# P times V as fp32 products of two heads in different columns of the array, V kept whole in the place of the norm rows, and single banks for column products

## The chip, the cores and the metric

The kernel runs on one core of a Trainium2 chip. The metric is the device time of one execution in microseconds (us); lower is better. The engines are TensorE (PE, with its weight loads PEld), VectorE (DVE), ScalarE (ACT), GpSimd (POOL) and the DMA queue of SyncE (SP). SBUF is the on-chip memory, PSUM the small memory into which PE writes; PSUM has eight banks here of 512 fp32 values in each of 128 partitions.

## The reference

Two layers on 256 tokens of width 1024, all in fp32. Layer 0 mixes tokens with a gated MLP (gMLP), layer 1 with attention in 16 heads of 64; after each mixer comes a gated MLP with a causal convolution of width 3 (ConvFFN, width 2816). Every part ends in `x <- LayerNorm(alpha * x + f(x))`. Since one attention block holds 256 tokens, attention sees its own block alone: plain causal attention with a bias by distance.

```python
def chunked_gmlp(x, w_in, ln_g, ln_b, w_s, b_s, w_out):
    z = jax.nn.gelu(x @ w_in)
    u, v = jnp.split(z, 2, axis=-1)
    v = layer_norm(v, ln_g, ln_b)
    ...
    sv = jnp.einsum('gts,bnsgc->bntgc', w, v) + b_s.T[None, None, :, :, None]
    return (u * sv.reshape(B, S, GMLP_WIDTH)) @ w_out
...
        p = jax.nn.softmax(logits, axis=-1)
        ...
        return (jnp.einsum('bhqjl,bhqjld->bhqd', p_sel, v_sel)
                + jnp.einsum('bhql,bhld->bhqd', p_own, v_own))
    ...
    return o @ w_o

def conv_ffn(x, w_up, conv_w, conv_b, w_down):
    h = x @ w_up
    ...
    return (jax.nn.gelu(g) * val) @ w_down
```

## The kernel before

**Products in parts.** An fp32 matrix is cut into a high part in the rounded type fp32r and a low part, the rest. ACT makes the high part by a copy (line 338 of the profile, `act`), DVE the low part by a subtraction (line 344, `tt`); `split` records both. A product is then three fp32r products: high by high, high by low, low by high (line 326, `mms`). Small products are done in plain fp32 without parts: gMLP's spatial products and the part of the scores that needs it. In the trace an fp32 product shows as two records. Transposes are on line 332.

**Weights** arrive in chunks of 1 MB by SP (line 355), two raw places and five chunks ahead (`prep`, `spent`); a chunk is loaded when the one five before it is spent. ACT and DVE split each chunk into `whi` and `wlo`.

**The order of work.** The class `Plan` records every operation with its engine, an assumed duration and what it depends on, and then lists them for each engine by due times. The main products keep the order in which they are recorded; operations with `fill=True` (spatial products, scores, transposes, P times V) are slipped in as soon as they are ready. `plan.later(ns, fn)` records something only when PE's recorded work has gone on by so many ns; the constant `REST` does so with the last part of a layer norm (`rest` in `ln_back`: times and plus the norm rows), whose rows `lnrow` are loaded by `ln_rows` into a single place (`rowring`).

**PSUM.** Four banks are tiles of their own, `bank0` to `bank3`; the other four are the halves of two double tiles, `twos0` and `twos1`. `bank()` gives the oldest free single bank (a half of a double tile if none is free), `half()` a half of the double tile that was used longest ago, `couple(j)` names both halves of tile j, `taken(i, long)` takes a certain one. Dependences are kept per tile: a product into one half of a double tile waits for readers of the other half.

**Stages.** gMLP: v by rows, then u in eight groups g of 24 column products (`cols_times`, 256 columns each; the result is 128 features by 256 tokens) read by ACT's gelu; three groups later `spatial(g)`, two fp32 products of 128 columns in a half, read by DVE. Then a_out, the ConvFFN f_up0 and f_dn0 (`project_out`). Attention (`moba`): V by rows into the two couples, then for each pair i of heads (i = 0 to 7) `project(i, 0)` for Q and `project(i, 1)` for K, 24 column products each in a half; `scores(i - 1)`, two heads in different rows of the array (64 each), an fp32 product of 128 columns and three fp32r products of 256 for each head; `softmax`, whose first step is four DVE reads of the scores with the bias (line 825); `turn(i - 2)`, three transposes of P for each head; `apply(i - 3)`, P times V. Here P and V are both split, P's parts lie in `rr`; three products of 512 columns take both heads' P against 128 features of V, and three of 256 columns the second half of the tokens, so of the 128 by 512 result only each head's own 64 rows count. Two splits of 64 partitions take them out for b_o. Behind the last pair b_o and the second ConvFFN follow.

Of the kernel before, what the change touches and what calls it, by code (L numbers as in the profile page):

```python
# [13 lines left out]
AF = mybir.ActivationFunctionType  # L14
# [4 lines left out]
P = 128  # L19
D = 1024  # L20
# [25 lines left out]
T1_WAITS = (2600, 3300, 4000, 4700)  # L46
REST = 25000
AHEAD = 12000
# [175 lines left out]
def trunk_kernel(ctx: ExitStack, tc: tile.TileContext, a: dict, out: bass.AP):  # L224
# [64 lines left out]
    def couple(j):  # L289
        return j + BANKS // 2, j + BANKS // 2 + len(twos)  # L290
# [227 lines left out]
    def ln_back(r, st, mean, rstd, rows, t, li, h, l, waits):  # L518
# [16 lines left out]
        def turn(k0):  # L535
            pt, x32 = bank(), (x32a if step == 4 else x32b).new()
            transposes([(pt.ap[:, j * P:(j + 1) * P], x[:, (k0 + j) * P:(k0 + j + 1) * P]) for j in range(step)],
                       [(r, range(k0 // 2, (k0 + step) // 2))], [pt])
            for j in range(step):
                k = k0 + j  # L540
                act(x32.ap[:, j * P:(j + 1) * P], pt.ap[:, j * P:(j + 1) * P], AF.Identity, [pt, lncol], [(x32, [j])],
                    bias=lc[:, li, 1, k:k + 1], scale=lc[:, li, 0, k:k + 1], psum=True)
            parts = [(t, k) for k in range(k0, k0 + step)]
            split((h, parts, xt_view(h)[:, t, k0:k0 + step, :]), (l, parts, xt_view(l)[:, t, k0:k0 + step, :]),
                  (x32, range(step), x32.ap.rearrange("p (k c) -> p k c", k=step)))
            if k0 + step == KT:
                plan.later(REST, rest)

# [34 lines left out]
    def project_out(name, nk, at, xold, li, rows_i):  # L583

        rows = ln_rows(rows_i)
        last = li is None


# [17 lines left out]
        for t in range(NT):  # L606
# [17 lines left out]
            if t == NT - 1:  # L624
                for k in range(start, nk, 2):
                    spent(name, k // 2)

            st, mean, rstd = stats(r, x, cuts[t], lambda j, o, n: add(*mine[j], 1.0 if mine[j] in ends else ALPHA))
            if last:
# [9 lines left out]
    def gmlp():  # L639
# [37 lines left out]
        for g in range(GROUPS):  # L677
            b = half()
            cols_times(b, xh, xl, *sub("a_u", g // 2, g % 2))
# [78 lines left out]
    def moba(h, l, scr):  # L758
        n4 = KT * S
        oh, ol = place("rr", 0, n4), place("rr", n4, n4)  # L760
        vh, vl = place("rr", 2 * n4, NT * D), place("rr", 2 * n4 + NT * D, NT * D)
        pw = 2 * (P + S)
        pring = [Places("rr", [4 * n4 + (2 * j + x) * pw for x in range(2)], pw) for j in range(2)]
        qkring = [Places("ff", (j * 2 * P, j * 2 * P + P), P) for j in range(2)]
# [3 lines left out]
        ohv, olv = (b.ap.rearrange("p (k s) -> p k s", k=KT) for b in (oh, ol))  # L768
        vhv, vlv = (b.ap.rearrange("p (t d) -> p t d", t=NT) for b in (vh, vl))
        at = xt_at(h, l)  # L770
        pieces = [[(o, HALF, taken(i, True)) for o, i in zip((0, HALF), couple(j))] for j in range(NT)]
        for ks in (range(5), range(5, KT)):
            for t in range(NT):
# [6 lines left out]
                if ks[0]:  # L780
                    for o, n, b in pieces[t]:
                        parts = [(t, i) for i in range(o // P, (o + n) // P)]
                        split((vh, parts, vhv[:, t, o:o + n]), (vl, parts, vlv[:, t, o:o + n]), (b, [0], b.ap), psum=True)
                        done_with(b)
        held, biases = {}, {}

        def project(i, j):
            b, t = half(), qkring[j].new()
            cols_times(b, h, l, *sub("b_qk", i, j))
# [15 lines left out]
        def scores(i):  # L805
            ((q0, qh, ql), (k0, kh, kl)), bias = held[i], biases[i]
            bank2 = [bank() for _ in range(2)]

# [29 lines left out]
        def turn(i):  # L838
            ph, pl = (x.new() for x in pring)
            for hh in range(2):  # L840
                e, b = held[i][hh], bank()

                transposes([(b.ap[:, c * P:(c + 1) * P], e.ap[:, c * P:(c + 1) * P]) for c in range(3)],
                           [(e, [0, 1])], [b])
                sl = slice(hh * (P + S), (hh + 1) * (P + S))
                split((ph, [hh], ph.ap[:, sl]), (pl, [hh], pl.ap[:, sl]), (b, [0], b.ap[:, :P + S]), psum=True)
            held[i] = ph, pl

        def apply(i):
            ph, pl = held[i]  # L850
            b = bank()
            o3 = b.ap.rearrange("p (a b) -> p a b", a=2)
            vs = slice(i * P, (i + 1) * P)
            seq = [(vhv, ph), (vhv, pl), (vlv, ph)]
            w = [(o3, v[:, 0, vs], p.ap.rearrange("p (a s) -> p a s", a=2)[:, :, :S], j == 0, False)
                 for j, (v, p) in enumerate(seq)]
            w += [(o3[:, :, P:], v[:, 1, vs], p.ap.rearrange("p (a s) -> p a s", a=2)[:, :, S:], False, j == 2)
                  for j, (v, p) in enumerate(seq)]
            mms(w, [(vh, [(0, i), (1, i)]), (vl, [(0, i), (1, i)]), (ph, [0, 1]), (pl, [0, 1])], [b], fill=True)
            for hh in range(2):  # L860
                hs = slice(hh * DH, (hh + 1) * DH)
                split((oh, [(i, hh)], ohv[hs, i, :]), (ol, [(i, hh)], olv[hs, i, :]), (b, [0], o3[hs, hh, :]), psum=True)

# [108 lines left out]
```

## Time and profile before

| what | us |
|---|---|
| median of 3 executions | 578.51 (577.9 to 579.87) |
| the profiled execution | 579.16 |
| its span, first to last instruction | 577.5 |
| PE busy | 560.1 (97% of the span) |
| PEld busy | 485.9 |
| DVE busy | 473.7 |
| ACT busy | 361.9 |

The profile is of one execution. A row of the timeline gives the start, the duration, the engine, the line, what is written and read, and in brackets how long the engine was idle ahead of it and what ended that; neighbours of the same kind are joined (x2, x3). Ends of products on PE are modelled and overlap the next start, so steps are read from start to start. The granted clock was 0.997 of full speed on the mean. All times in the text are us from the start of the span, unless said otherwise.

### The profile page before, as it was taken

To read this page: it belongs to the slowest core of one execution; us is meant where nothing else is said; L and a number is where in the kernel's file an instruction comes from. 1 tells how busy PE (TensorE), PEld (TensorE's weight loads), DVE (VectorE), ACT (ScalarE), POOL (GpSimd) and SP (SyncE) were. 2 spreads that over 40 slices of the span, in tenths; PEclk is the share of its full clock that TensorE was granted. 3 is DMA by queue.
4 is the path that set the end of the run, shared out by engine and by line. 5 is a ranking of instruction groups with operands and counts; after the bars stand their busy time and mean duration, and the time that the engine had idled before them with its cause. 6 is when DMAs were issued, how large, how long until landed. Compare 5 with 4: busy or idle time off the path is not lost.

```text
span 577.5 us, 8559 instructions
## 1 busy us (share of the span) xinstructions
PE 560.1 (97%) x3210; PEld 485.9 (84%) x3210; DVE 473.7 (82%) x885; ACT 361.9 (63%) x660; POOL 11.3 (2%) x17
## 2 busy tenths in 40 slices
PE   6998999999999999999999999999999999999994
PEld 4798888888888878888889998888888888888884
DVE  5587989999999997558878889879999999996426
ACT  5555567776677685435568777658777778785300
POOL 0020010000000000001000000000000000000001
PEclk9999999999999999999999999999999999999998
DMA  7887544537454567742663442515456555567202
GB/s 260 330 336 274 199 145 151 215 145 259 188 211 156 210 230 267 259 169 87 250 250 117 181 165 92 201 73 183 183 188 254 199 170 211 219 218 255 110 1 73
DMA packets 20133, 110.93 MB, mean 192 GB/s; under 512 B 2251, under 2 KB 6268, under 8 KB 7676
## 3 DMA queue, kind: packets, MB, share of 16 engines
q1 hardware_dynamic: 20092, 110.39, 53.0%
q8 instruction: 25, 0.41, 0.3%
q14 instruction: 16, 0.13, 0.1%
HBM read 109.31 MB, written 1.07 MB: 191 GB/s over the span
## 4 chain that ended last, share of the span: by engine, by line
PE 92%; DVE 3%; DMA 2%; ACT 2%; issue 0%; SPq 0%; DVEq 0%; ACTq 0%
PE twos L326 60%; PE bank L326 29%; DMA raw<-in_a_v 2%; PE bank L332 2%; DVE wlo L344 1%; DVE rr L344 1%; ACT ff L338 1%; DVE x L348 0%; ACT whi L338 0%; ACT rr L338 0%; SPq L355 0%; DVE ff L825 0%; PE twos L332 0%; DVE ff L834 0%; DVE stat L494 0%
## 5 line engine op out<-in xcount | busy, mean ns | idle before, releaser
L326 PE MATMUL twos<-xt,whi 128*128 128x512 f32 (+1 forms) x1024 | 295.1, 354 | 2.0 <-ACT ff L338 1.5
L344 DVE TENSOR_TENSOR wlo<-raw,whi 128x1024 fp32r<-128x1024 f32 (+1 forms) x212 | 228.4, 1098 | 30.8 <-ACT whi L338 30.3
L326 PE MATMUL twos<-xt,wlo 128*128 128x256 f32 x832 | 231.5, 278 | 0.0
L338 ACT ACTIVATE whi<-raw 128x1024 fp32r<-128x1024 f32 (+1 forms) x212 | 195.0, 954 | 56.7 <-DMA raw<-in_f_up 18.2
L326 PEld LDWEIGHTS twos<-xt,whi 128*128 128x128 f32 x1024 | 179.5, 189 | 31.7 <-ACT ff L338 2.4
L326 PEld LDWEIGHTS twos<-xt,wlo 128*128 128x128 f32 x832 | 156.8, 188 | 0.1
L326 PE MATMUL bank<-whi,rr 128*128 128x512 f32 x432 | 135.2, 391 | 0.4 <-DVE smax L825 0.4
L326 PEld LDWEIGHTS bank<-whi,rr 128*128 128x128 f32 x432 | 81.1, 188 | 18.0 <-issue 0.6
L326 PE MATMUL bank<-wlo,rr 128*128 128x512 f32 x216 | 84.1, 389 | 0.0
L348 DVE SCALAR_TENSOR_TENSOR ff<-ff,convc 128x255 f32<-128x255 f32 (+1 forms) x160 | 69.1, 477 | 0.0
L338 ACT ACTIVATE ff<-twos 128x512 f32<-128x512 f32 (+2 forms) x64 | 31.4, 491 | 53.4 <-PE twos L326 52.6
L326 PEld LDWEIGHTS bank<-wlo,rr 128*128 128x128 f32 x216 | 40.6, 188 | 8.1
L338 ACT ACTIVATE ff<-ff,convc 128x256 f32<-128x256 f32 x80 | 45.5, 592 | 2.9 <-DVE ff L344 2.5
L344 DVE TENSOR_TENSOR ff<-twos,ff 128x512 f32<-128x512 f32 (+1 forms) x48 | 30.9, 645 | 16.0 <-ACT ff L338 11.7
L326 PE MATMUL twos<-whi,xt 128*128 128x512 f32 x128 | 42.1, 396 | 0.5 <-DVE x L348 0.5
L338 ACT ACTIVATE ff<-bank,lncol 128x128 f32<-128x128 f32 x48 | 18.9, 460 | 29.1 <-PE bank L332 28.4
L348 DVE SCALAR_TENSOR_TENSOR x<-x,bank 128x512 f32<-128x512 f32 x16 | 11.0, 686 | 23.7 <-PE bank L326 23.6
L326 PEld LDWEIGHTS twos<-whi,xt 128*128 128x128 f32 x128 | 24.1, 188 | 5.7 <-DVE x L348 0.9
L326 PE MATMUL bank<-whi,xt 128*128 128x512 f32 x64 | 21.9, 420 | 5.1 <-DVE xt L361 5.0
L338 ACT ACTIVATE rr<-ff 128x256 fp32r<-128x256 f32 x52 | 21.0, 406 | 7.4 <-DVE ff L344 7.4
L326 PE MATMUL twos<-wlo,xt 128*128 128x512 f32 x64 | 25.0, 390 | 0.0
L344 DVE TENSOR_TENSOR ff<-ff 128x256 f32<-128x256 f32 x52 | 21.6, 418 | 0.5 <-ACT ff L338 0.2
(67 smaller groups left out, 416.9 us busy)
## 6 DMA issues: line engine op xcount, KB each, us to landing
raw<-in_f_up SPq DMA_DIRECT2D x44, 1024.0 KB, 4.8
raw<-in_f_dn SPq DMA_DIRECT2D x22, 1024.0 KB, 4.8
raw<-in_b_qk SPq DMA_DIRECT2D x8, 1024.0 KB, 4.8
lnrow<-in_lnrow SPq DMA_DIRECT2D x5, 1024.0 KB, 6.7
raw<-in_a_u SPq DMA_DIRECT2D x4, 1024.0 KB, 5.3
raw<-in_a_out SPq DMA_DIRECT2D x4, 1024.0 KB, 4.9
raw<-in_b_v SPq DMA_DIRECT2D x4, 1024.0 KB, 4.8
raw<-in_b_o SPq DMA_DIRECT2D x4, 1024.0 KB, 4.8
```

The lines of the kernel that those rows point to most:

```text
L326: nc.tensor.matmul(o, l, x, start=start, stop=stop)
L332: nc.tensor.transpose(o, x, ident.ap)
L338: plan.op("act", ns, lambda: nc.scalar.activation(o, x, func, **kw), r, w, table=table)
L344: dve(70 + 1.04 * flat(x), lambda: nc.vector.tensor_tensor(o, x, y, op=op), r, w)
L348: lambda: nc.vector.scalar_tensor_tensor(o, x, s, y, op0=op0, op1=op1), r, w)
```

## The change

gMLP's groups of column products and Q's and K's take `bank()` in place of `half()`. Scores of a pair take the two halves of twos0, the transposed P those of twos1, and the six transposes of a pair are one operation of the plan. V's couples are taken in the order in which they come free. V stays fp32: one copy by ACT in the place of the norm rows (`vb = rowring.new()`), no low part. P too: one copy by ACT in places of `ff`. P times V is four fp32 products: for each head 64 features of V by its own P, head 0 into partitions 0 to 63 and head 1 into 64 to 127, that is, in different columns of the array; 256 tokens for the first 128 keys and 128 tokens for the second. The result is split once for both heads. Since V lies in the norm rows' place, b_o's rows are loaded only when V is done with, and the rest of f_dn0's layer norm is recorded after 9000 ns in place of 25000.

```diff
-REST = 25000
+REST = 25000, 9000, 25000
...
-                plan.later(REST, rest)
+                plan.later(REST[li], rest)
...
-        rows = ln_rows(rows_i)
         last = li is None
+        rows = None if name == "b_o" else ln_rows(rows_i)
...
+            rows = rows or ln_rows(rows_i)
             st, mean, rstd = stats(r, x, cuts[t], lambda j, o, n: add(*mine[j], 1.0 if mine[j] in ends else ALPHA))
...
         for g in range(GROUPS):
-            b = half()
+            b = bank()
             cols_times(b, xh, xl, *sub("a_u", g // 2, g % 2))
...
-        vh, vl = place("rr", 2 * n4, NT * D), place("rr", 2 * n4 + NT * D, NT * D)
-        pw = 2 * (P + S)
-        pring = [Places("rr", [4 * n4 + (2 * j + x) * pw for x in range(2)], pw) for j in range(2)]
+        pring = Places("ff", [4 * P, 19 * S, 19 * S + P + S, 19 * S + 2 * (P + S)], P + S)
...
-        vhv, vlv = (b.ap.rearrange("p (t d) -> p t d", t=NT) for b in (vh, vl))
+        vb = rowring.new()
+        vv = vb.ap.rearrange("p (t d) -> p t d", t=NT)
         at = xt_at(h, l)
-        pieces = [[(o, HALF, taken(i, True)) for o, i in zip((0, HALF), couple(j))] for j in range(NT)]
+        free_first = sorted(range(NT), key=lambda j: max(bank_of[i][0] for i in couple(j)))
+        pieces = [[(o, HALF, taken(i, True)) for o, i in zip((0, HALF), couple(j))] for j in free_first]
...
-                        split((vh, parts, vhv[:, t, o:o + n]), (vl, parts, vlv[:, t, o:o + n]), (b, [0], b.ap), psum=True)
+                        act(vv[:, t, o:o + n], b.ap, AF.Copy, [b], [(vb, parts)], psum=True)
...
-            b, t = half(), qkring[j].new()
+            b, t = bank(), qkring[j].new()
             cols_times(b, h, l, *sub("b_qk", i, j))
...
-            bank2 = [bank() for _ in range(2)]
+            bank2 = [taken(x, False) for x in couple(0)]
...
-            ph, pl = (x.new() for x in pring)
-            for hh in range(2):
-                e, b = held[i][hh], bank()
...
-                split((ph, [hh], ph.ap[:, sl]), (pl, [hh], pl.ap[:, sl]), (b, [0], b.ap[:, :P + S]), psum=True)
-            held[i] = ph, pl
+            bs = [taken(x, False) for x in couple(1)]
+
+            transposes([(b.ap[:, c * P:(c + 1) * P], e.ap[:, c * P:(c + 1) * P])
+                        for e, b in zip(held[i], bs) for c in range(3)], [(e, [0, 1]) for e in held[i]], bs)
+            for hh, b in enumerate(bs):
+                p = pring.new()
+                act(p.ap, b.ap[:, :P + S], AF.Copy, [b], [p], psum=True)
+                held[i][hh] = p
...
-            seq = [(vhv, ph), (vhv, pl), (vlv, ph)]
-            w = [(o3, v[:, 0, vs], p.ap.rearrange("p (a s) -> p a s", a=2)[:, :, :S], j == 0, False)
-                 for j, (v, p) in enumerate(seq)]
-            w += [(o3[:, :, P:], v[:, 1, vs], p.ap.rearrange("p (a s) -> p a s", a=2)[:, :, S:], False, j == 2)
-                  for j, (v, p) in enumerate(seq)]
-            mms(w, [(vh, [(0, i), (1, i)]), (vl, [(0, i), (1, i)]), (ph, [0, 1]), (pl, [0, 1])], [b], fill=True)
-            for hh in range(2):
-                hs = slice(hh * DH, (hh + 1) * DH)
-                split((oh, [(i, hh)], ohv[hs, i, :]), (ol, [(i, hh)], olv[hs, i, :]), (b, [0], o3[hs, hh, :]), psum=True)
+            w = [(b.ap[hh * DH:(hh + 1) * DH, at:S], vv[:, c, i * P + hh * DH:i * P + (hh + 1) * DH],
+                  held[i][hh].ap[:, cut], c == 0, c == 1)
+                 for c, (at, cut) in enumerate(((0, slice(0, S)), (P, slice(S, S + P)))) for hh in range(2)]
+            mms(w, [(vb, [(0, i), (1, i)]), *held[i]], [b], fill=True)
+            both_heads = [(i, hh) for hh in range(2)]
+            split((oh, both_heads, ohv[:, i, :]), (ol, both_heads, olv[:, i, :]), (b, [0], b.ap[:, :S]), psum=True)
```

Three places show how the order moves. In the rows a number stands behind each tile's name (`twos0_105` is the tile twos0), and x2 joins neighbours.

The first is PE in gMLP, around the second group of u's column products (weights whi0 and whi1) and the spatial products (`ff_104`). Before:

```order
L326 MATMUL twos0_105<-xt_87,wlo0_75 128x256
L326 MATMUL twos0_105<-ff_104 128x128 x2
L326 MATMUL twos0_105<-xt_87,whi0_65 128x256 x2
L326 MATMUL twos0_105<-xt_87,wlo0_75 128x256
L326 MATMUL twos1_106<-xt_87,whi1_66 128x256 x2
L326 MATMUL twos1_106<-xt_87,wlo1_76 128x256
```

And now:

```order
L326 MATMUL bank2_109<-xt_87,wlo0_75 128x256
L326 MATMUL twos0_105<-ff_104 128x128 x2
L326 MATMUL twos1_106<-ff_104 128x128 x2
L326 MATMUL bank3_110<-xt_87,whi1_66 128x256 x2
L326 MATMUL bank3_110<-xt_87,wlo1_76 128x256
```

Column products and spatial products no longer share a tile; the groups go round the four single banks.

The second is PE at the end of attention: the transposes of pair 6 or 7 (L332), scores(7) (`qk...`), P times V of pair 6 (`rr_103` alone before, `lnrow0_90` after) and the first products of b_o (`whi4_69,rr_103`). Before:

```order
L332 MATMUL bank1_108<-ident_111,ff_104 128x128 x3
L326 MATMUL bank2_109<-ff_104 128x128
...
L326 MATMUL bank3_110<-qk25601_121,qk12811_119 128x256
L326 MATMUL twos0_105<-rr_103 128x512 x3
L326 MATMUL twos0_105<-rr_103 128x2x128 x3
L326 MATMUL bank2_109<-whi4_69,rr_103 128x512
```

And now:

```order
L332 MATMUL twos1_106<-ident_111,ff_104 128x128 x6
L326 MATMUL bank0_107<-whi4_69,rr_103 128x512
...
L326 MATMUL twos0_105<-ff_104 128x128 x2
...
L326 MATMUL twos0_105<-qk25601_121,qk12811_119 128x256 x2
L326 MATMUL bank2_109<-whi4_69,rr_103 128x512
...
L326 MATMUL bank3_110<-whi4_69,rr_103 128x512
L326 MATMUL twos0_105<-ff_104,lnrow0_90 64x256 x2
L326 MATMUL twos0_105<-ff_104,lnrow0_90 64x128 x2
```

Three of b_o's products into each of bank0 and bank1 now stand ahead of scores(7), three into each of bank2 and bank3 between them and P times V of pair 6, which goes into the tile that scores(7) wrote.

The third is SP's queue. Before, b_o's norm rows are loaded among Q's and K's chunks:

```order
L355 DMA raw0_85<-in_b_qk 128x2048
L355 DMA lnrow0_90<-in_lnrow 128x2048
L355 DMA raw1_86<-in_b_qk 128x2048
L355 DMA raw0_85<-in_b_qk 128x2048
L355 DMA ff_104<-rbscr_115 128x2x256
```

Now they stand among the first chunks of f_up1:

```order
L355 DMA raw1_86<-in_f_up1 128x2048
L355 DMA raw0_85<-in_f_up1 128x2048
L355 DMA raw1_86<-in_f_up1 128x2048
L355 DMA lnrow0_90<-in_lnrow 128x2048
L355 DMA raw0_85<-in_f_up1 128x2048
```

The load moved behind the third chunk of f_up1.

## Rows read from the trace of the kernel before

**Rows 1.** The page, part 1: busy us (share of the span) xinstructions of each engine

```profile
PE 560.1 (97%) x3210; PEld 485.9 (84%) x3210; DVE 473.7 (82%) x885; ACT 361.9 (63%) x660; POOL 11.3 (2%) x17
```

**Rows 2.** By stretch: length, then PE, PEld, DVE, ACT, POOL busy, clock, DMA share, GB/s

```profile
20.00:60.00 40.00, 38.16 (x267) 35.14 (x268) 31.54 (x50) 23.39 (x33) 3.50 (x3) 1.00 0.83 309
301.00:350.00 49.00, 49.00 (x412) 46.61 (x412) 42.44 (x140) 37.82 (x108) 0.00 (x0) 1.00 0.44 154
```

**Rows 3.** Timeline of PE in gMLP, u's column products and two spatial products

```profile
43.92 0.28 PE L326 MATMUL twos<-xt,wlo 128*128 128x256 f32 x1
44.68 0.50 PE L326 MATMUL twos<-xt,whi 128*128 128x256 f32 x2 [0.47 <-ACT ff L338]
...
52.55 0.61 PE L326 MATMUL twos<-ff 128*128 128x128 f32 x4
53.25 0.50 PE L326 MATMUL twos<-xt,whi 128*128 128x256 f32 x2
```

**Rows 4.** PE's waits from 31 to 62 us: total us, times, longest

```profile
PE twos L326 <- ACT ff L338: 1.5, 3, 0.5
```

**Rows 5.** The chain from 43 to 62 us: start, us, what

```profile
52.81 0.39 ACT ff L338
...
61.59 0.44 PE twos L326 x4
```

**Rows 6.** Timeline of PE: the start of V's product, the start of Q's

```profile
270.44 0.50 PE L326 MATMUL twos<-whi,xt 128*128 128x512 f32 x1 [0.51 <-DVE x L348]
...
296.28 0.50 PE L326 MATMUL twos<-xt,whi 128*128 128x256 f32 x2 [0.40 <-DVE rr L344]
```

**Rows 7.** Timeline of PE: scores(7), P times V of pair 6, the start of b_o

```profile
358.01 0.49 PE L326 MATMUL bank<-ff 64*128 64x128 f32 x4 [0.57 <-ACT ff L338]
...
359.38 1.32 PE L326 MATMUL twos<-rr 128*128 128x512 f32 x6
361.10 0.51 PE L326 MATMUL bank<-whi,rr 128*128 128x512 f32 x1 [0.40 <-DVE smax L825]
```

**Rows 8.** Timeline of PE: scores(0), P times V of pair 0, and their neighbours

```profile
300.93 0.28 PE L326 MATMUL twos<-xt,wlo 128*128 128x256 f32 x1
301.14 0.49 PE L326 MATMUL bank<-ff 64*128 64x128 f32 x4
301.38 0.61 PE L326 MATMUL bank<-qk,qk 64*128 64x256 f32 x6
301.92 0.51 PE L326 MATMUL twos<-xt,whi 128*128 128x256 f32 x2
...
310.80 1.22 PE L326 MATMUL bank<-rr 128*128 128x512 f32 x6
311.85 0.40 PE L326 MATMUL twos<-xt,whi 128*128 128x256 f32 x2
```

**Rows 9.** Groups by line, 301 to 361 us: busy us, mean ns, idle before, releaser

```profile
L344 DVE TENSOR_TENSOR rr<-bank,rr 128x384 fp32r<-128x384 f32 (+1 forms) x26 | 12.3, 491 | 1.9 <-ACT rr L338 1.6
```

**Rows 10.** Timeline of DVE: first and last of four reads of scores(7)

```profile
360.41 0.42 DVE L825 CUSTOM_DVE_ANT_0 ff<-bank,ff 128x256 f32<-128x256 f32 x1
...
361.31 0.28 DVE L825 CUSTOM_DVE_ANT_0 ff<-bank,ff 128x128 f32<-128x128 f32 x1
```

**Rows 11.** Timelines of DVE, ACT, SP and DVE: norm rows, V's copy, f_up1's third load

```profile
285.87 0.68 DVE L344 TENSOR_TENSOR x<-x,lnrow 128x512 f32<-128x512 f32 x1
...
288.97 0.60 ACT L338 ACTIVATE rr<-twos 128x512 fp32r<-128x512 f32 x1 [4.84 <-PE twos L326]
...
369.78 0.33 SPq L355 DMA_DIRECT2D raw<-in_f_up  x1
...
382.25 1.28 DVE L344 TENSOR_TENSOR x<-x,lnrow 128x512 f32<-128x512 f32 x2
```

**Rows 12.** The page, part 6: KB each, median us from issue to landing

```profile
lnrow<-in_lnrow SPq DMA_DIRECT2D x5, 1024.0 KB, 6.7
```

**Rows 13.** Groups by line, 301 to 361 us: weight loads of P times V

```profile
L326 PEld LDWEIGHTS bank<-rr 128*128 128x128 f32 x36 | 6.0, 189 | 0.8
```

More of the change, by code (lines that the diff above doesn't have):

```diff
@@ L838, in turn @@
         def turn(i):
-            ph, pl = (x.new() for x in pring)
-            for hh in range(2):
-                e, b = held[i][hh], bank()
-                transposes([(b.ap[:, c * P:(c + 1) * P], e.ap[:, c * P:(c + 1) * P]) for c in range(3)],
-                           [(e, [0, 1])], [b])
-                sl = slice(hh * (P + S), (hh + 1) * (P + S))
-                split((ph, [hh], ph.ap[:, sl]), (pl, [hh], pl.ap[:, sl]), (b, [0], b.ap[:, :P + S]), psum=True)
-            held[i] = ph, pl
+            bs = [taken(x, False) for x in couple(1)]
[5 more added lines that the diff above has]
+                held[i][hh] = p
         def apply(i):
-            ph, pl = held[i]
             b = bank()
-            o3 = b.ap.rearrange("p (a b) -> p a b", a=2)
-            vs = slice(i * P, (i + 1) * P)
-            seq = [(vhv, ph), (vhv, pl), (vlv, ph)]
-            w = [(o3, v[:, 0, vs], p.ap.rearrange("p (a s) -> p a s", a=2)[:, :, :S], j == 0, False)
-                 for j, (v, p) in enumerate(seq)]
-            w += [(o3[:, :, P:], v[:, 1, vs], p.ap.rearrange("p (a s) -> p a s", a=2)[:, :, S:], False, j == 2)
-                  for j, (v, p) in enumerate(seq)]
-            mms(w, [(vh, [(0, i), (1, i)]), (vl, [(0, i), (1, i)]), (ph, [0, 1]), (pl, [0, 1])], [b], fill=True)
-            for hh in range(2):
-                hs = slice(hh * DH, (hh + 1) * DH)
-                split((oh, [(i, hh)], ohv[hs, i, :]), (ol, [(i, hh)], olv[hs, i, :]), (b, [0], o3[hs, hh, :]), psum=True)
+            w = [(b.ap[hh * DH:(hh + 1) * DH, at:S], vv[:, c, i * P + hh * DH:i * P + (hh + 1) * DH],
[4 more added lines that the diff above has]
+            split((oh, both_heads, ohv[:, i, :]), (ol, both_heads, olv[:, i, :]), (b, [0], b.ap[:, :S]), psum=True)
         for i in range(PAIRS):
```

## The prediction

> **What bounds the kernel now.** I read the page's first part first: TensorE (PE) is busy 560.1 us of a span of 577.5 [rows 1]. So time is won in two ways only: PE gets less to do, or one of its short stops goes. The table by stretch shows which of the two a stage can give [rows 2]. Between 301 and 350 us, where attention runs for seven of its eight head pairs, PE is busy 49.00 of 49.00 us while DVE has 42.44 and ACT 37.82: what the change takes from DVE and ACT there is worth nothing, and only PE's own microseconds count. Between 20 and 60 us PE is busy 38.16 of 40.00, so there are stops; they are found in PE's timeline, its waits and the chain [rows 3 to 5]. The rest comes from PE's timeline around 270, 296 and 357 us [rows 6, 7], and the prices of the attention products from one visit of each kind [rows 8].
>
> The profiled execution took 579.16 us (the span of 577.5 and 1.66 outside it), 0.65 over 578.51, the median of the three runs. The sum is made against 579.16, and 0.65 is taken off at the end.
>
> **Part 1: banks of gMLP's column products.** When a group of column products ends in its half of a twos tile, the next product writes the other half of the same tile, and PE stands until ACT's gelu has read the first half. Undisturbed, 2,304 columns pass in 1.05 (310.80 to 311.85) [rows 8], so 256 in 0.12. The product at 44.68 started 0.76 after the one at 43.92 [rows 3]: 0.64 late, although the row names 0.47 of idle. A stop thus costs about 0.17 more than its printed idle. The waits list three such stops, 1.5 us together [rows 4]: 1.5 + 3 x 0.17 = 2.0 us. A fourth hides behind the two fp32 products at 52.55: 0.70 to the next start [rows 3] where the same two take 0.44 elsewhere, with ACT's gelu in the chain between [rows 5]; that is 0.26. After each of the four restarts the first pair lasts 0.50 against 0.40 [rows 3, 8], which is 0.4. In the new order column products go round bank0 to bank3, and the spatial products between them alternate between the two twos tiles, so a single bank is written again only after three other groups of 24 products of 0.12, some 9 us. A spatial product now needs DVE's read of the one two back, which is six or more steps of three products (2.2 us) away. **Gain 2.0 + 0.26 + 0.4 = 2.67.** What is late next would be weights: DMA is busy 0.83 of that stretch at 309 GB/s [rows 2]. If the stream has no slack, all 2.67 come back as waits at a_out. Its loads start when chunks are spent, so they move up with PE, and I take nothing off.
>
> **Part 2: the couples of V's product, and Q's bank.** At 270.44 PE waited 0.51 for DVE, which was still adding to x from the other half of the tile [rows 6]; with 0.17 and 0.10 as above that is 0.78. The new order starts with the couple whose bank was taken earlier. At 296.28 the first product of Q waited 0.40 for DVE's low part of V in the same tile [rows 6]: 0.40 + 0.17 + 0.10 = 0.67, and Q now goes to a single bank. **Gain 1.45**; nothing, at the low end, if the last read of the older couple is as late. With V and P unsplit and the result split once for both heads, DVE loses 4 + 16 + 8 subtractions of some 0.5 us each [rows 9]; these 14 us lie beside a busy PE and count nothing here.
>
> **Part 3: the end of attention.** With the projections done, PE has little to put beside pair 7 [rows 7]. Scores(7) at 358.01 waited 0.57 for ACT's copy of K, with the 0.17 as above some 0.7. The scores take 1.37 (358.01 to 359.38) where they took 0.78 (301.14 to 301.92) earlier [rows 8], since the low parts of Q and K come late: 0.59. P times V of pair 6 starts at 359.38 and lasts 1.05, so b_o could start at 360.43 and starts at 361.10, because its bank holds scores that DVE is reading: 0.67, and 0.11 for the restart. Together 2.07. In the new order the first row of b_o (six products of 512 columns at 0.23, 1.4 us in two halves) stands around scores(7), and scores have twos0, so these three stops have cover. But P times V of pair 6 now goes to twos0 too, behind DVE's four reads of the scores. These took 1.19 (360.41 to 361.59), and began 1.03 after the scores' end, behind a subtraction [rows 10]; between scores(7) and that product stand six products, 1.4 us. The new wait lies between nothing (DVE free at once) and 1.03 + 1.19 - 1.4 = 0.8; I take the middle, 0.4. **Gain 2.07 - 0.4 = 1.7.**
>
> **Part 4: P times V.** Before, six fp32r products took 1.05. After, four fp32 products: two of 256 columns in the left and the right half of the array, then two of 128. An fp32 product of 128 columns takes 0.22 (two in 0.44 [rows 5]), one of 256 by that 0.44. In turn the four are 2 x 0.44 + 2 x 0.22 = 1.32; side by side 0.66. No row shows two products in different columns. The nearest are the scores, two heads in different rows: two fp32 and six fp32r products that in turn would take 0.44 + 6 x 0.12 = 1.16, side by side 0.58, and that took 0.78 [rows 8]. So they do run side by side, 0.20 over the half; the start is 0.09 late (301.14 against 300.93 + 0.12), and the first pair behind lasts 0.51 against 0.40. A visit to the divided array costs 0.20 + 0.09 + 0.11 = 0.40 over its work, and P times V becomes 0.66 + 0.40 = 1.06 against 1.05. **Gain nothing, eight times**, between 0.66 (no cost of a visit: 8 x 0.39 = 3.1 gained) and 1.32 + 0.40 = 1.72 (in turn: 8 x 0.67 = 5.4 lost).
>
> The rows show 0.40 for going into the divided array and back. The Trainium skill, page "TensorEngine Tiling (Array Packing)", section Key Properties, says that changing the tiling mode drains TensorE; the rows agree. Its page "TensorE: Matmul & The Clock Gate", section Measured speedup vs the span model, gives packed products the time of one product and about 4 ns for each further tile; by that rule P times V would be 0.66 and the sum 3.1 lower, which is rival (a). No run here shows it yet, and the scores' 0.20 over the half speaks against it.
>
> **Part 5: the layer norm rows.** V stands in their place, so V's copies need f_dn0's last read of them: in the old order that is DVE's at 285.87, and ACT's first copy of V starts at 288.97 [rows 11]; the change records that rest 16 us of PE's line earlier. b_o's rows are loaded once P times V of pair 7 is done, behind the third load of f_up1, issued at 369.78 [rows 11]. Landing takes 6.7 [rows 12], so about 377; the next reader on DVE was at 382.25 [rows 11]. Some 5 us of cover; without it DVE stands with the splits of xt queued behind the reader, and PE with them. The f_up1 loads behind it on SP come 1 MB later.
>
> **Sum.** 2.67 + 1.45 + 1.7 + 0 = 5.8. 579.16 - 5.8 = 573.4 against the profiled execution, 572.7 against the median.
>
> **The rivals.** (a) **Free switching**: P times V takes 0.66, 572.7 - 3.1 = 569.6. Against: the scores' 0.40. (b) **In turn**: the columns do not overlap, since both heads' P pass through all rows of the array, which the scores (each head its own rows) never did. 572.7 + 5.4 = 578.1, no change. For it: no row shows otherwise. (c) **gMLP's gain is given back** at a_out, where the stream at 0.83 has little slack: 572.7 + 2.67 = 575.4. Against: the waits of that stretch list no stop for DMA or splits. (d) **Slower**: in turn, and each of the eight records of a visit (an fp32 product shows as two) waits for its own weight load, which now lies beside the product before. A load lasts 0.189 [rows 13]; 8 x 0.19 = 1.5 more, 1.32 + 0.40 + 1.5 = 3.2 per visit, 2.17 x 8 = 17.4 lost: 590.1. It ends slower from a visit of 1.05 + 5.8 / 8 = 1.78 on. Against: the scores are short products with loads of their own and show no such thing. (e) That PE waits for the banks as before is excluded by the order, save for the wait in part 3.
>
> **How the numbers follow.** Forecast 572.7, chance 0.52, own range 571.2 to 574.2 (part 3's wait 0.4 either way, and 0.14 on each of eight visits). Free switching 0.14, in turn 0.19, gain given back 0.07, slower 0.08. A measurement of this kernel can tell about 0.3%, 1.7 us, from no change, so faster ends at 576.8: forecast, free switching and gain given back are faster, 0.73, and 0.01 of in turn; the rest of that is the same but for 0.02 over 580.2. Faster 0.74, same 0.16, slower 0.10. The range from 569.5 to 578.5 leaves out the slower rival and the edges.
>
> **What would show it.** Between 31 and 62 us PE's waits for ACT's ff are gone; at 270 and 296 us PE has no stop. P times V has eight visits of about 1.06 from start to the next start: 0.7 or 1.7 brings down part 4 and decides between forecast, (a), (b) and (d). Before the product of pair 6 PE waits for DVE's reads of the scores, up to 0.8. DVE's busy time falls by some 14 us with nothing to show for it. The prediction is wrong if PE waits at a_out, or if DVE waits for lnrow near 380 us.

## The result: 573.31 us, 1.1% faster

The changed kernel takes 573.31 us in the median of six executions, the kernel before 578.93 beside it. One of the six took 1128.57, which nothing here explains; the other five lie between 571.67 and 573.82 with a median of 572.98, and they alone give the ratio 0.9893, 95% interval 0.987 to 0.9915, which is 6.2 us (4.9 to 7.5). The profiled execution took 573.82, its span 572.1 (before 577.5).

The page, part 1 (answers to rows 1) and the first line of part 4, by engine:

```profile
PE 557.8 (98%) x3226; PEld 482.7 (84%) x3226; DVE 459.9 (80%) x857; ACT 356.0 (62%) x652; POOL 11.5 (2%) x17
...
PE 91%; DMA 4%; DVE 2%; SPq 1%; ACT 0%; issue 0%; DVEq 0%
```

DVE lost 13.8 us of work, PE's busy time fell by 2.3. All waits of PE that the trace of after names (line, releaser, us in total, times, longest):

```profile
PE bank L326 <- DVE xt L361: 5.0, 1, 5.0
PE bank L326 <- DVE wlo L344: 1.3, 2, 0.8
PE twos L326 <- DVE ff L348: 0.2, 1, 0.2
```

The first two belong to the start of the kernel. The stops behind ACT's ff and DVE's x, rr and smax [rows 3, 4, 6, 7] are gone, and with them one more that PE's waits of the kernel before list, in scores(7) behind the low part of K or Q:

```profile
PE bank L326 <- DVE qk L348: 0.3, 1, 0.3
```

One of 0.2 behind DVE's ff is new. The table by stretch says the same of attention (columns as in rows 2):

```profile
289.00:348.00 59.00, 59.00 (x505) 54.45 (x503) 43.77 (x134) 43.61 (x115) 0.00 (x0) 1.00 0.53 191
348.00:364.00 16.00, 16.00 (x113) 12.82 (x112) 13.06 (x46) 11.33 (x35) 0.00 (x0) 1.00 0.36 133
```

PE stands nowhere in it, not even at its end. To see where the time went I cut each trace at the starts of five products on PE: u's first column product, the first product of ConvFFN 0, V's first, Q's first, the first of ConvFFN 1. In after they are:

```profile
32.11 0.28 PE L326 MATMUL bank<-xt,whi 128*128 128x256 f32 x1
...
82.33 0.40 PE L326 MATMUL twos<-whi,xt 128*128 128x512 f32 x1
...
268.00 0.40 PE L326 MATMUL twos<-whi,xt 128*128 128x512 f32 x1
...
290.71 0.28 PE L326 MATMUL bank<-xt,whi 128*128 128x256 f32 x1
...
380.52 0.40 PE L326 MATMUL twos<-whi,xt 128*128 128x512 f32 x1
```

The lengths between them (us), from the trace of every run of this study:

| run | start of u | gMLP from u on | ConvFFN 0 | V | Q to b_o |
|---|---|---|---|---|---|
| before | 31.29 | 52.11 | 185.67 | 23.78 | 93.06 |
| after | 32.11 | 50.22 | 185.67 | 22.71 | 89.81 |
| x1_gmlp_banks | 31.85 | 49.47 | 185.67 | 23.80 | 93.02 |
| x5_no_free_first | 31.46 | 49.47 | 185.67 | 23.77 | 89.74 |
| x6_attention_banks | 29.44 | 52.11 | 185.67 | 22.75 | 91.61 |
| x4_low_parts_back | 29.68 | 49.47 | 185.67 | 22.72 | 90.95 |
| x12_p_low_parts_back | 31.84 | 49.47 | 185.67 | 22.69 | 90.22 |
| x3_full_array | 31.77 | 49.47 | 185.67 | 22.73 | 92.66 |
| x2_same_columns | 29.72 | 49.47 | 185.67 | 22.75 | 95.00 |
| x10_head_by_head | 30.93 | 49.47 | 185.67 | 22.71 | 89.84 |
| x9_scores_with_apply | 29.58 | 49.47 | 185.67 | 22.73 | 89.59 |
| x11_tail_apart | 30.75 | 49.47 | 185.67 | 22.73 | 89.41 |
| x13_twos1 | 30.44 | 49.47 | 185.67 | 22.75 | 88.51 |

But for gMLP in after (below), stretches whose code is the same agree to 0.08 us between runs, so a stretch tells tenths where a median tells one or two us. The one column that scatters is the first: u starts between 29.44 and 32.11 although nothing ahead of it differs. Waits of PE for the low parts of weights are a part of it: 1.3 in after, none named in x2, which starts at 29.72. The 5.4 us of the two spans are 1.89 of gMLP, 1.07 of V and 3.25 of attention, less 0.82 by which this execution started late.

### The profile page after: what moved, and what is told of

Same layout as the page of the kernel before. It is cut to its first block, busy times and chain, and to the rows that moved or that the text cites. A ratio compares the mean times of both kernels' runs of the same rounds, so it can differ in the third digit from the quotient of the medians.

```text
span 572.1 us, 8555 instructions
## 1 busy us (share of the span) xinstructions
PE 557.8 (98%) x3226; PEld 482.7 (84%) x3226; DVE 459.9 (80%) x857; ACT 356.0 (62%) x652; POOL 11.5 (2%) x17
## 3 DMA queue, kind: packets, MB, share of 16 engines
HBM read 109.31 MB, written 1.07 MB: 193 GB/s over the span
## 4 chain that ended last, share of the span: by engine, by line
PE 91%; DMA 4%; DVE 2%; SPq 1%; ACT 0%; issue 0%; DVEq 0%
PE twos L326 52%; PE bank L326 38%; DMA raw<-in_a_v 2%; DMA raw<-in_a_u 2%; DVE wlo L344 1%; PE bank L332 1%; PE twos L332 1%; SPq L355 1%; ACT whi L338 0%; DVE x L348 0%; DVE ff L348 0%; DVE stat L494 0%; DVEq L964 0%; DVE stat L497 0%; DVE stat L499 0%
## 5 line engine op out<-in xcount | busy, mean ns | idle before, releaser
L326 PE MATMUL twos<-xt,whi 128*128 128x512 f32 x640 | 222.2, 394 | 0.0
L326 PE MATMUL twos<-xt,wlo 128*128 128x256 f32 x640 | 177.3, 277 | 0.0
L326 PEld LDWEIGHTS twos<-xt,whi 128*128 128x128 f32 x640 | 120.0, 188 | 27.7
L326 PEld LDWEIGHTS twos<-xt,wlo 128*128 128x128 f32 x640 | 120.2, 188 | 0.1
L326 PE MATMUL bank<-xt,whi 128*128 128x256 f32 x384 | 71.8, 288 | 0.0
L348 DVE SCALAR_TENSOR_TENSOR ff<-ff,convc 128x254 f32<-128x254 f32 (+1 forms) x160 | 69.7, 478 | 0.5 <-ACT ff L338 0.2
L326 PEld LDWEIGHTS bank<-xt,whi 128*128 128x128 f32 x384 | 59.6, 191 | 2.0 <-issue 1.0
L338 ACT ACTIVATE ff<-twos 128x512 f32<-128x512 f32 (+1 forms) x56 | 31.0, 567 | 46.3 <-PE twos L326 43.9
L326 PE MATMUL bank<-xt,wlo 128*128 128x256 f32 x192 | 54.2, 282 | 0.0
L326 PEld LDWEIGHTS bank<-xt,wlo 128*128 128x128 f32 x192 | 36.7, 191 | 0.0
```

Source lines behind the costliest of these rows:

```text
L326: nc.tensor.matmul(o, l, x, start=start, stop=stop)
L338: plan.op("act", ns, lambda: nc.scalar.activation(o, x, func, **kw), r, w, table=table)
L348: lambda: nc.vector.scalar_tensor_tensor(o, x, s, y, op0=op0, op1=op1), r, w)
```

## Experiments on the banks

**One line for gMLP.** The kernel before with

```diff
-            b = half()
+            b = bank()
             cols_times(b, xh, xl, *sub("a_u", g // 2, g % 2))
```

> The kernel before with one line of the change: gMLP's column products in single banks. Theory (the stops on a shared double tile are the cost): the stretch from u's first product to the first product of the next ConvFFN, 52.1 us before, gets shorter by 1.9 (as in the changed kernel) to 2.7, everything behind it keeps its length, total about 576.5. Rival (the weight stream sets this stretch, the gain comes back as waits for weights): the stretch keeps 52.1 and the time stays at 578.5.

576.61 us (575.15 to 577.06), ratio 0.9944 (0.9927 to 0.9961). gMLP is 52.11 - 49.47 = 2.64 shorter, no other stretch moves. The stops on the shared tile were the whole of it, and the weight stream takes nothing back.

Every run with these banks has 49.47, only the profiled execution of after has 50.22. It is the one with the latest start. Of the 0.75, 0.49 stand at the spatial products at 41.35 and 0.27 at the next ones at 45.88. PE's timeline there:

```profile
40.74 0.39 PE L326 MATMUL twos<-ff 128*128 128x128 f32 x2
41.35 0.94 PE L326 MATMUL twos<-ff 128*128 128x128 f32 x6 [0.22 <-DVE ff L348]
```

And DVE's in the same execution:

```profile
39.67 1.22 DVE L344 TENSOR_TENSOR wlo<-raw,whi 128x1024 fp32r<-128x1024 f32 x1
40.81 0.48 DVE L348 SCALAR_TENSOR_TENSOR ff<-ff,stat,lnrow 128x256 f32<-128x256 f32 x1
```

A spatial product waits for the layer norm of v, which stands on DVE behind the low part of a chunk. In x12, whose u starts only 0.27 earlier, DVE comes to the same layer norm 2.79 earlier:

```profile
38.02 0.48 DVE L348 SCALAR_TENSOR_TENSOR ff<-ff,stat,lnrow 128x256 f32<-128x256 f32 x1
```

So DVE's line is late as a whole in the profiled execution of after: the chain has a chunk of a_u that lands at 31.52 ahead of it, and one low part that takes 2.1 where others take 1.22. The spatial products, earlier by the gain, meet it. Whether this happens in the other executions of the changed kernel is not known.

**The order of V's couples.** The changed kernel with

```diff
-        free_first = sorted(range(NT), key=lambda j: max(bank_of[i][0] for i in couple(j)))
+        free_first = range(NT)
```

> The changed kernel with V's couples in the fixed order twos0, twos1 again. Theory (V's stretch lost its stop to the order of the couples alone): V's stretch 1.0 longer, 23.8 in place of 22.7, with a wait of PE for DVE's sum into x of about 0.5, and nothing else moves: total 574.4. Rival (the earlier rest of the layer norm and the unsplit V removed the stop): 22.7 and no wait.

573.2 us of two executions (573.05 and 573.36). V's stretch is 23.77 again, the others stay, and the stop is back where rows 6 had it. PE's timeline:

```profile
267.97 0.50 PE L326 MATMUL twos<-whi,xt 128*128 128x512 f32 x1 [0.52 <-DVE x L348]
```

The order of two couples is worth 1.06 us by itself; the earlier rest of the layer norm and V without low parts, which x5 keeps, give this stretch nothing. Its median alone would not have shown it.

**Attention's banks without the fp32 products.** The kernel before with the change's lines for V's couples, `bank()` in `project`, `couple(0)` in `scores`, and in `turn`

```diff
-                e, b = held[i][hh], bank()
-                transposes([(b.ap[:, c * P:(c + 1) * P], e.ap[:, c * P:(c + 1) * P]) for c in range(3)],
-                           [(e, [0, 1])], [b])
+            bs = [taken(x, False) for x in couple(1)]
+            transposes([(b.ap[:, c * P:(c + 1) * P], e.ap[:, c * P:(c + 1) * P])
+                        for e, b in zip(held[i], bs) for c in range(3)], [(e, [0, 1]) for e in held[i]], bs)
```

> The kernel before with only the PSUM part of the attention change: the older couple first for V, single banks for Q and K, scores in twos0, transposed P in twos1 by six transposes at once. V and P are split and P times V is six fp32r products as before. Theory (the stops go with the banks, DVE's and ACT's relief is worth nothing): V's stretch 1.1 shorter, from Q's first product to b_o's last 2.7 shorter, total about 574.8. Rival (the stops go because DVE and ACT have less to do): the stops at K's start and at the end of attention stay, at least 1.5 of the 3.8 is missing, total 576.5 or more.

575.37 us (574.84 to 576.77), ratio 0.9935 (0.9919 to 0.995); the profiled execution, 574.84, has the earliest start of all. V's stretch gains 1.03 as expected, attention 1.45 and not 2.7. The stops for K's bank and for the scores are gone, and the one that the prediction had put at up to 0.8 has come, P times V of pair 6 behind DVE's reads of scores(7). PE's timeline:

```profile
357.57 0.40 PE L326 MATMUL bank<-whi,rr 128*128 128x512 f32 x1
358.18 1.31 PE L326 MATMUL twos<-rr 128*128 128x512 f32 x6 [0.21 <-DVE smax L826]
```

0.61 from start to start where 0.23 is the step: 0.38 late. The changed kernel has no such wait. Most of what is missing stands at P times V: pair 4 (341.92) starts 0.17 late, with a weight load that waited 0.21 for DVE's qk, and five of the eight pairs take 1.10 to 1.16 in place of 1.05; with the 0.38 that is 1.0 of 1.25. So neither side was right: the banks by themselves carry less than half of attention's gain, and a part of the rest needs a DVE that is on time.

## Experiments on DVE's relief

**All low parts put back.** The changed kernel with `split` for V, P and the two halves of the result, whose low parts of V and P nobody reads. Of P:

```diff
-                act(p.ap, b.ap[:, :P + S], AF.Copy, [b], [p], psum=True)
+                pl = plring.new()
+                split((p, [0], p.ap), (pl, [0], pl.ap), (b, [0], b.ap[:, :P + S]), psum=True)
```

> The changed kernel with DVE's work put back that the change took away: low parts of V and P are computed again (by nobody read) and the result is split in two halves of 64 partitions, about 14 us more on DVE and 3 on ACT. Products, banks and order of the groups stay. Theory (relief of DVE and ACT is worth nothing): within 0.5 us of the changed kernel, with the end of attention the one place where up to 0.5 may be lost. Rival (the relief carries a part of the gain): slower by 1.5 or more, with new stops of PE behind DVE in attention.

572.6 us (571.8 to 574.68), no slower than the changed kernel by its median; but its profiled execution started 2.4 earlier, and attention is 90.95 against 89.81: 1.14 longer. PE's waits in this kernel have two new lines (one more belongs to the start):

```profile
PE bank L326 <- DVE qk L348: 0.3, 1, 0.3
PE twos L326 <- DVE smax L830: 0.2, 1, 0.2
```

The first of them on DVE's timeline:

```profile
321.73 0.55 DVE L344 TENSOR_TENSOR rr<-twos,ff 128x384 fp32r<-128x384 f32 x1
322.20 0.16 DVE L833 TENSOR_SCALAR smax<-smax 128x2 f32<-128x2 f32 x1
322.27 0.55 DVE L344 TENSOR_TENSOR rr<-twos,ff 128x384 fp32r<-128x384 f32 x1
322.82 0.29 DVE L348 SCALAR_TENSOR_TENSOR qk<-bank,qk 128x128 fp32r<-128x128 f32 x1
```

And on PE's:

```profile
322.57 0.28 PE L326 MATMUL bank<-xt,wlo 128*128 128x256 f32 x1
323.17 0.87 PE L326 MATMUL bank<-ff,lnrow 128*64 128x256 f32 x8 [0.32 <-DVE qk L348]
```

Two subtractions of P (0.55 each) stand in DVE's line ahead of the low part of Q or K, and P times V takes the bank from which that is read: 0.39 late. The second wait makes P times V of pair 6 late by 0.29 more than in the changed kernel, and another P times V (331.72) starts 0.08 late. But this run changes more than DVE's work: the plan, which orders by assumed durations, lists the groups a little otherwise. In the changed kernel P times V of pair 5 (347.95) stands right behind scores(6) and shares their visit to the divided array; in x4 three products stand between (PE's timeline):

```profile
344.72 0.50 PE L326 MATMUL bank<-xt,whi 128*128 128x256 f32 x2
...
345.26 0.87 PE L326 MATMUL bank<-ff,lnrow 128*64 128x256 f32 x8
```

That is one visit more, some 0.2 of the 1.14. So the relief of DVE, with 3.6 us less on ACT (356.0 against 359.6), is worth 0.9 to 1.1 us in the new order, although in the changed kernel DVE is busy only 43.77 of 59.00 us there.

**Only P's low parts.** The same without V's and with the result split once.

> The changed kernel with only the low parts of P computed again (16 subtractions, read by nobody), not those of V and not the two halves of the result. Theory (with all three put back attention was 1.1 longer by two waits, for the low part of Q or K and for the reads of scores(7), and DVE's subtractions of P stand ahead of both): 90.9 again, both waits. Rival (the two halves of the result, which hold PSUM longer, made them): 89.8, no wait.

573.72 us (573.15 and 574.29). Attention is 90.22, 0.41 longer, and PE's waits name neither place; P times V of pair 6 is late by 0.26 (a step of 0.49 for 0.23), too little for the list, where the changed kernel has 0.09. Neither side: P's subtractions alone cost a third of the 1.14. The plan sets P times V of pair 2 six products later here than in x4, so that the first of the two places is not the same; and x4's extra visit is not there. What the halves of the result cost was not tried by itself: their share stays open.

## Experiments on P times V

Three kernels change how the four fp32 products of a visit (the P times V of one pair, for which PE's array is divided) are laid out. In the whole array, each head's P by the features of both heads:

```diff
-            w = [(b.ap[hh * DH:(hh + 1) * DH, at:S], vv[:, c, i * P + hh * DH:i * P + (hh + 1) * DH],
+            w = [(o3[:, hh, at:S], vv[:, c, i * P:(i + 1) * P],
```

Both heads in the left half:

```diff
-            w = [(b.ap[hh * DH:(hh + 1) * DH, at:S], vv[:, c, i * P + hh * DH:i * P + (hh + 1) * DH],
+            w = [(o3[:DH, hh, at:S], vv[:, c, i * P + hh * DH:i * P + (hh + 1) * DH],
```

And one head behind the other, in the change's columns:

```diff
-                 for c, (at, cut) in enumerate(((0, slice(0, S)), (P, slice(S, S + P)))) for hh in range(2)]
+                 for hh in range(2) for c, (at, cut) in enumerate(((0, slice(0, S)), (P, slice(S, S + P))))]
```

The first two also take the products head by head and split the result in two halves, since both heads' results lie side by side in the bank (`o3`).

> The changed kernel with the same unsplit V and P, but each head's P is multiplied by the 128 features of both heads in the whole array, so nothing runs side by side and the array isn't divided; the other head's rows are not used. Theory (columns run side by side, 0.80 from start to next start and 0.19 around it): a visit is 1.30 plus 0.08, so 0.4 longer, 8 times: 3.1 slower than the changed kernel, about 576.5. Rival (the time of a visit is hidden or the columns give nothing): no difference from the changed kernel, 573.3.

> The changed kernel with both heads' products in the left half of the array (columns 0 to 63), so that they can only run in turn, and the result taken out in two halves. Theory (the gain of the visit is the overlap of the two halves): 2 x 0.43 + 2 x 0.22 = 1.30 from start to next start in place of 0.80, with the same 0.19 around it: attention 8 x 0.5 = 4 us longer than in the changed kernel (93.8 in place of 89.8), total about 577. Rival (half as many columns make each product shorter, overlap has no part in it): 0.80 and 89.8 as before.

> The changed kernel with the four products of P times V in another order: both of head 0, then both of head 1, still in different columns. Theory (PE takes products in order and runs two at once only if neighbours go to different columns): the second product of head 0 and the first of head 1 overlap, 0.43 + 0.43 + 0.22 = 1.08 in place of 0.80: attention 2.2 us longer, 92.0. Rival a (the halves run independently whatever the order): 0.80, 89.8. Rival b (every change of the half ends the overlap): 1.30, 93.8.

One visit of each on PE's timeline, with the product ahead and the pair behind. After:

```profile
309.73 0.28 PE L326 MATMUL bank<-xt,wlo 128*128 128x256 f32 x1
309.94 0.87 PE L326 MATMUL bank<-ff,lnrow 128*64 128x256 f32 x8
310.74 0.50 PE L326 MATMUL bank<-xt,whi 128*128 128x256 f32 x2
```

x3_full_array:

```profile
308.65 0.28 PE L326 MATMUL bank<-xt,wlo 128*128 128x256 f32 x1
308.77 1.47 PE L326 MATMUL bank<-ff,lnrow 128*128 128x256 f32 x8
310.00 0.48 PE L326 MATMUL bank<-xt,whi 128*128 128x256 f32 x2
```

x2_same_columns:

```profile
306.63 0.28 PE L326 MATMUL bank<-xt,wlo 128*128 128x256 f32 x1
306.84 1.51 PE L326 MATMUL bank<-ff,lnrow 128*64 128x256 f32 x8
308.28 0.51 PE L326 MATMUL bank<-xt,whi 128*128 128x256 f32 x2
```

x10_head_by_head:

```profile
307.79 0.28 PE L326 MATMUL bank<-xt,wlo 128*128 128x256 f32 x1
308.00 0.88 PE L326 MATMUL bank<-ff,lnrow 128*64 128x256 f32 x8
308.81 0.50 PE L326 MATMUL bank<-xt,whi 128*128 128x256 f32 x2
```

From start to next start: 0.80 in different columns, 1.23 in the whole array, 1.44 in the same columns. In the whole array the visit starts on the step (0.12), in columns 0.09 late (0.21). No wait of PE stands in attention in any of them, so the halves of the result cost them nothing that the list shows. The groups stand in x10 as in the change, and in x3 and x2 too, but for the end, where scores(7) and what follows it come three products earlier. Attention follows: 92.66 for x3 (2.85 longer, 3.1 expected; 574.7 us, 573.76 to 575.55, ratio 0.9919, 0.9904 to 0.9934) and 95.00 for x2 (5.2 longer, which is 8 x 0.64, where 4 was expected with 1.30 for a visit; 577.22 us, 575.9 to 578.06, ratio 0.9972, 0.9958 to 0.9985). Products in different columns run at the same time; half as many columns alone shorten nothing, since x2 has them too and pays the visit to the divided array without the overlap. x2 also shows the change without overlap: by its ratio 1.6 of 6.2 us would be left. For x10 my theory fell: 0.81 and 89.84, so the second head's products start beside the first head's although they come behind them in the code (573.53 us, two executions). Rival a holds. The records say the same: in x2, with the same order in the code, they come in that order, 256 columns, 128, 256, 128; in x10 all four of 256 columns start by 308.28, ahead of the four of 128, which start from 308.49 on.

## One step further

A visit to the divided array costs 0.09 at its start and a long first pair behind it. Scores and P times V of two different pairs can share one visit, as scores(6) and pair 5 happen to do in the changed kernel; as one operation of the plan they always do:

```diff
-            mms(both((0, P), [(q0, k0)]) + both((P, P + S), [(qh, kh), (qh, kl), (ql, kh)]),
-                [q0, qh, ql, k0, kh, kl], bank2, fill=True)
+            seq, r, done = apply(j) if j is not None else ([], [], None)
+            mms(both((0, P), [(q0, k0)]) + both((P, P + S), [(qh, kh), (qh, kl), (ql, kh)]) + seq,
+                [q0, qh, ql, k0, kh, kl] + r, bank2 + ([done[1]] if done else []), fill=True)
```

> The changed kernel with one step more: for six of the eight pairs P times V is put into the same operation as the scores of the pair two later, so that PE visits the divided array once where it did twice. Theory (a visit costs 0.19 to 0.25 for going in and out, seen as a late start and a long first product): 0.19 less for the five visits that were apart, attention about 88.9 in place of 89.8, total about 572.4. Rival (going from rows to columns costs as much as going out and in): 89.8, no change; worse if P times V now waits for the scores' inputs and its result comes late for b_o.

571.33 us (570.3 to 574.0), ratio 0.9882 (0.9859 to 0.9905), but attention is only 0.22 shorter: at its end P times V of pair 6 waits again for the scores' reads, which are now late. PE's timeline:

```profile
352.50 0.39 PE L326 MATMUL bank<-whi,rr 128*128 128x512 f32 x1
353.31 0.87 PE L326 MATMUL twos<-ff,lnrow 128*64 128x256 f32 x8 [0.42 <-DVE smax L830]
```

With the end left as in the change:

> The kernel with scores and P times V in one operation, but at the end of attention, where it brought a wait of 0.42 for DVE's reads of scores(7), both stand apart as in the changed kernel. Theory (a shared visit saves 0.19, the loss was that wait): attention 0.7 to 0.9 shorter than the 89.8 of the changed kernel, about 89.0, no wait for the scores' reads; total 572 or a little under, as the start falls. Rival (sharing a visit saves nothing): 89.8.

571.3 us (570.33 to 572.34), ratio 0.9864 (0.9841 to 0.9887), attention 89.41: 0.40 shorter, and the wait is there all the same. My reading of where it came from fell: it is not the shared visit at the end. In x11 DVE's reads of scores(7) begin at 353.29, 0.82 behind the scores' end, behind two low parts of a weight chunk (1.29 together); in the changed kernel they begin 0.11 behind it. Why the low parts stand there was not traced. Of PE's waits:

```profile
PE twos L326 <- DVE smax L830: 0.4, 1, 0.4
```

So the wait itself was removed: P times V of pair 6 goes to a half of twos1, whose last readers are ACT's copies of the same pair's P, which it needs anyway.

```diff
-        plan.later(2500, lambda: apply(n - 1))
+        plan.later(2500, lambda: apply(n - 1, True, taken(couple(1)[0], False)))
```

> The kernel with scores and P times V in one operation throughout, and P times V of pair 6 in a half of twos1, which that pair's own transposes leave, and not in twos0 behind DVE's reads of scores(7). Theory (the wait of 0.42 printed, 0.6 in all, was the shared tile's, and the shared visits save 0.19 each): attention 0.8 to 1.0 shorter than the 89.8 of the changed kernel, 88.8 to 89.0, no wait for the scores' reads, total 571 give or take the start. Rival (the wait only changes its name: P times V of pair 6 now stands right behind its transposes and waits for ACT's copies of P): 89.5, with a wait of PE for ACT of about 0.4.

570.5 us (569.39 to 571.39) with the kernel before at 578.79 beside it, ratio 0.9859 (0.9837 to 0.9881). Attention is 88.51, 1.30 shorter than in the change; PE waits for neither the scores' reads nor ACT. Nine visits to the divided array are left of fifteen, so a visit saved gave 0.22. The scores, P times V of pair 5 and that of pair 6 now stand in one visit (its first part on PE's timeline):

```profile
350.51 0.49 PE L326 MATMUL twos<-ff 64*128 64x128 f32 x4
350.76 0.61 PE L326 MATMUL twos<-qk,qk 64*128 64x256 f32 x6
351.30 0.87 PE L326 MATMUL bank<-ff,lnrow 128*64 128x256 f32 x8
```

That is the fastest kernel here, by the stretch 1.3 us under the changed one; the two were not timed beside each other.

## Why the prediction was right, and where not

The forecast of 572.7 lies 0.6 from the median of six and 0.3 from that of the five. That it is so close is in part luck. By stretches, with the gMLP stretch of all other runs, the change is worth 2.64 + 1.07 + 3.25 = 7.0, against 5.8 in the sum; the interval of the ratio, 4.9 to 7.5, holds both, since starts differ from execution to execution by up to 2.7. The sum had 2.67 for gMLP, 0.78 for V and 0.67 + 1.7 + 0 = 2.37 for attention, where 3.25 was measured: the 0.9 between are the wait of 0.4 that did not come and a visit that was priced too high. Point by point:

- **Part 1**, 2.67: 2.64, shown by x1_gmlp_banks alone. The rival that it is given back at a_out did not happen there; in the profiled execution 0.75 came back at another place, DVE's layer norm of v, that I had not named.
- **Part 2**, 0.78 for V: 1.07, the order of the couples by itself (x5). The 0.3 more stand at eight transposes of x (L332) in this stretch, beside DVE's last writes of x: 1.05 from start to next start before (274.00 to 275.05), 0.71 after, 1.04 in x5. The stop at 296.28 I had called Q's; Q's first product starts at 292.85, and it is K's. Its mechanism and size do not change by that, and its wait is gone.
- **Part 2**, DVE's relief counts nothing: wrong by 0.9 to 1.1 us (x4). I had read it from the old order, in which PE stood nowhere between 301 and 350 us [rows 2]. The new order puts products on banks that DVE has just to read, and there a subtraction more or less in DVE's line decides.
- **Part 3**, 2.07 less a new wait of 0.4: the wait is real (0.21 printed in x6, 0.22 in x4, 0.42 in x9) but the changed kernel does not have it. PE's timeline at that place of after, which answers to rows 7:

```profile
355.31 0.49 PE L326 MATMUL twos<-ff 64*128 64x128 f32 x4
355.55 0.61 PE L326 MATMUL twos<-qk,qk 64*128 64x256 f32 x6
356.09 0.50 PE L326 MATMUL bank<-whi,rr 128*128 128x512 f32 x1
...
357.38 0.39 PE L326 MATMUL bank<-whi,rr 128*128 128x512 f32 x1
357.70 0.87 PE L326 MATMUL twos<-ff,lnrow 128*64 128x256 f32 x8
```

  The scores take 0.78 and the step to P times V is 0.32, which is the 0.23 and the 0.09 of a visit. I had taken the middle of 0 to 0.8 with DVE's line as it was before, where the reads began 1.03 behind the scores' end. DVE's first and last read in after:

```profile
356.20 0.29 DVE L827 CUSTOM_DVE_ANT_0 ff<-twos,ff 128x128 f32<-128x128 f32 x1
...
357.11 0.28 DVE L827 CUSTOM_DVE_ANT_0 ff<-twos,ff 128x128 f32<-128x128 f32 x1
```

  They take the same 1.19 but begin 0.11 behind the scores' end (356.09), and so are done 0.3 ahead of the product at 357.70.
- **Part 4**, 1.06 for 1.05: 0.80 + 0.09 and 0.10 for the long first pair, 0.99. The overlap and a cost of the visit like the scores' were right, the cost is 0.34 over 0.65 and not 0.40: 8 x 0.06 = 0.5 us more gain, and pair 5, which shares the visit of scores(6), saves some 0.2 beside. Free switching is ruled out by the same rows, and the products in turn by x2 and x3. By the rule of the Trainium skill, page "TensorE: Matmul & The Clock Gate", section Measured speedup vs the span model, a visit would have been 0.66; the trace shows 0.99, and the measurement decides. The slow rival needed 1.78 or more for a visit in all; even x2, in turn in the divided array, has 1.44 and 0.19 around it, 1.63, so PE does not wait 0.19 at each record for a load of its own.
- **Part 5**: nothing waits for the norm rows. In after the load is issued at 363.70 ahead of a chunk of f_up1 and lands 4.6 later, at 368.3, and DVE's next reader is at 376.86: 8.5 us of cover, where 5 were forecast from a later issue and a landing of 6.7.

```profile
363.70 0.33 SPq L355 DMA_DIRECT2D lnrow<-in_lnrow  x1
...
376.86 1.28 DVE L344 TENSOR_TENSOR x<-x,lnrow 128x512 f32<-128x512 f32 x2
```

Attention's 3.25 thus have three sources that lean on one another: banks by themselves 1.45 (x6), DVE's relief 0.9 to 1.1 (x4), and the columns with what is left, some 0.7 to 0.9. Against fp32 in the whole array the columns are worth 2.85 (x3), and without them dropping the parts would not pay: 92.66 in x3 against 91.61 in x6, which keeps them.

## What to carry to other kernels

Where the busiest engine is at 97%, look for tiles that two groups share: a stop for a reader of the other half costs the printed idle, some 0.17 more and a slow first pair, and one line can remove it. An engine that is idle a quarter of the time still sets the pace when a product is placed on a bank that it has just to read, so after a change of banks ask again who reads last. Cut traces at the same products and compare stretches: two tenths of a microsecond are plain there, where medians scatter by one or two with the first loads.

## What was not expected of the hardware

Two products in different halves of the columns run side by side whether they stand alternately in the code or one head behind the other (x10, 0.81 for a visit against 0.80). A product with 64 columns is no shorter than one with 128: the left half alone needs 1.44 for what the whole array does in 1.23, and record by record the steps are the same 0.22 and 0.11. Going from divided rows straight to divided columns and back to the whole array once costs about 0.22 less than two visits (x13, 1.30 us for six visits fewer).
